# Where the merge-gate blocks stand in a hybrid attention and mLSTM layer: beside attention, or behind the mLSTM

## The chip, the cores and the metric

The kernel runs on one core of one Trainium2 chip. The metric is the device time of one execution in microseconds; of several executions the median is given. Times below come from the profile of one execution, the rows of its trace, and the list of timed runs.

## What is computed

One trunk layer on 1024 prompt tokens and 32 sample tokens, together T = 1056, with D = 1024. The normalised input `h` is multiplied by one wide weight `w_in`; its columns are the attention's q, k, v (8 heads of 64), the mLSTM's q, k, v and output gate (4 heads of 128), eight scalar gates, and the two merge gates `ga` and `gm` of 1024 columns each:

```python
h = rmsnorm(x, g_mix) * (1 + sc1) + sh1
u = h @ w_in
qa, ka, va, qm, km, vm, om, ip, fp, ga, gm = jnp.split(u, _split_points(), axis=-1)
ya = band_attention(qa, ka, va, rel_bias)        # own 64-frame chunk and the 8 before
hm, (C1, n1, m1) = mlstm_chunkwise(q_m, k_m, v_m, log_i, log_f, C0, n0, m0, block)
ym = head_rmsnorm(hm, mh_gain) * jax.nn.sigmoid(om)
merged = jax.nn.sigmoid(ga) * (ya @ w_br_att) + jax.nn.sigmoid(gm) * (ym @ w_br_mlstm)
x = x + gt1 * (merged @ w_out)
```

A SwiGLU FFN and a final norm follow. `ga` and `gm` depend on `h` alone and are first used in the merge, so their columns can be computed at any time between the first norm and the merge.

## The kernel before

**Tiling.** `h` is held transposed in eight tiles of 128 channels x 1056 tokens. All products are done in fp32 split into a high and a low part: three passes (high x high, low x high, high x low), so a *block* of 128 output columns costs 8 x 3 matmuls for each of three token ranges of 352, 72 matmuls. `unit` (line 451) issues the 24 of one range; its matmuls are line 458. A block also loads 512 KB of weights on the SP queue (L434), splits them into high (ACT, L424) and low parts (L425), and empties three PSUM tiles (pool `mm`, three buffers) on ACT. The engine of the low split is chosen in `weight` (line 427 on): POOL until the second mLSTM has opened its output tile (`hm_n[1]`), DVE from then on. Weights are loaded and split ahead by the class `Weights`: up to two blocks split ahead, three more loaded.

**The order.** The order of the instructions on PE, ACT, DVE and POOL is that of the program's text; only DMA queues are ordered by the framework. A list `segs` (line 1330) holds segments; each has blocks, which are PE's steady filler, and at most one *side job*, a generator whose steps are put between the filler's matmuls. `unit` calls `side.tick()` after every second contraction slice, that is after every six matmuls, four ticks a unit and twelve a block. A job of n steps is spread evenly: `job = side.start(gen(), steps, ticks - delay - 4, delay)`, where `ticks` is 4 x the units of the segment's blocks, and `delay` is 13 from the sixth segment on (mLSTM and later) and 0 before. A step runs when its share of the ticks has come, whatever the engines do at that time. A second queue, `side.later`, holds short tails (transposes of k and v for their outputs, splits of the mLSTM's value weights), one of which is issued at each of three places in a unit.

**The segments.** The first computes k, v, q of head pair 0. In the next three, `attention(0)` to `attention(2)` run beside the blocks k, v, q of the next pair and beside merge-gate blocks: two, two and four of the sixteen. The fifth has `attention(3)` beside the mLSTM's first value block and four convolution blocks, the sixth the first half of the mLSTM beside five more, and the last has the second half of the mLSTM, the convolution's output rows and then `branch_operands` (sigmoid gating of the mLSTM output, split of both branches' operands) beside four output-gate blocks and the other eight merge-gate blocks. The merge follows. Another job, `ada_rest` (160 steps over 495 ticks from the second segment on), computes the later modulations on DVE (L1227, L1229), one tile of `w_ada` after the other.

**A step of attention.** `attention` (line 718) works on 18 items of one pair, two heads x (eight tiles of 128 queries and one sample tile), in 22 steps: one for the low part of the queries (L643, DVE), then a software pipeline. In a step, in this order: transposes of the item two back (PE, L774, tile `psT`) and their high part (ACT, L781); scores of the item (PE, L747, tile `psS`), the pass that adds the bias and takes the maximum (DVE, L761), the exponential (ACT, L762); the low part of the transposed item (DVE, L786); the reciprocal (DVE, L766) and the normalisation (POOL, L767); the values of the item three back (PE, L805, tile `psV`), and after each second item their sum (ACT L811, DVE L812 and L813). `psS`, `psT` and `psV` are one PSUM tile each, so the next transposes wait for the low part before, and the next scores for the pass before. The tiles are 128, 256, 384, 512 and then four times 640 keys wide, and 160 for the sample.

**A gate block.** `gate_block` (line 670) is one block whose three results go raw to a tile `t` (ACT, L677; a pool of four) and then by DMA to `g_d` in HBM (L678, SP). The merge reads them back (L1582, L1583) and takes the sigmoids.

**Slots.** Sixteen slots hold all the large tiles: eight are `h`; one each the cached keys and the low queries; k, q and v of each pair take three while their attention runs. `vm_block` (line 872) takes one for its raw weights and two for their parts, which four pieces on ACT (L888) and POOL (L889) fill from `side.later`.

Of the kernel before, what the change touches and what calls it, by code (L numbers as in the profile page):

```python
# [139 lines left out]
def hybrid_stream_step(  # L140
# [37 lines left out]
    def slot(shape, dt=F32):  # L178
        return slots.tile(shape, dt, tag="s", name=nm("s"))

    def tmpt(shape=(P, T), dt=F32):
        return tmp.tile(list(shape), dt, tag="t", name=nm("t"))

    def mmt():
        return mm.tile([P, 512], F32, tag="mm", name=nm("mm"))
# [236 lines left out]
    def split_to(dst, src, eng=dve):  # L422

        act.activation(dst[:, 0], src, AF.Copy)  # L424
        eng.tensor_tensor(dst[:, 1], src, f(dst[:, 0]), op=ALU.subtract)  # L425
# [25 lines left out]
    def unit(w, w0, xt, lo, hi, last=True):  # L451

        wt = W.use(w)
        pt = mmt()
        n = len(xt)
        for k in range(n):
            for q, (a, b) in enumerate(PASSES):
                pe.matmul(pt[:, :hi - lo], wt[(w0 + k) // 4][:, a, (w0 + k) % 4], xt[k][:, b, lo:hi],  # L458
                          start=(k == 0 and q == 0), stop=(k == n - 1 and q == 2))
            if k % 2 == 0 and k:  # L460
                side.flush(1)
            if k % 2 == 1:
                side.tick()
        if last:
            W.used(w)
        return pt[:, :hi - lo]
# [86 lines left out]
    def w_cols(c0, home=None):  # L553
        return weight([w_in[:, c0:c0 + P]], KD, 3, home)
# [4 lines left out]
    def k_block(hp):  # L559
        w = w_cols(KA + hp * P)  # L560

        def run():
            kt = att_k[hp] = slot([P, 2, T], F32R)
            kf = ap_.tile([P, T - 512], F32, tag="kf", name=nm("kf"), bufs=1)
            for lo, hi, pt in units(w):

                for hh, (u, v) in enumerate(ROWS):
                    act.activation(kt[u, hh, lo:hi], pt[u], AF.Copy)
                a = max(lo, 512)
                if a < hi:  # L570
                    act.activation(kf[:, a - 512:hi - 512], pt[:, a - lo:], AF.Copy)
                for hh, (u, v) in enumerate(ROWS):
                    dve.tensor_tensor(kt[v, hh, lo:hi], pt[u], f(kt[u, hh, lo:hi]), op=ALU.subtract)
            W.advance()
            side.later += [lambda: None, lambda: k_tail(hp, kf), lambda: sample_tail(kf[:, 512:], new_k_s, hp)]
        run.w = w
        return run
# [20 lines left out]
    def v_block(hp):  # L598
        w = w_cols(VA + hp * P)

        def run():
            vf = tmpt()
            if hp == 0:
                ckv = cache_loads()
            for lo, hi, pt in units(w):
                act.activation(vf[:, lo:hi], pt, AF.Copy)
            W.advance()
            side.later += [lambda: v_tail(hp, vf, 0), lambda: None, lambda: v_tail(hp, vf, 1), lambda: None,
                           lambda: v_sample(hp, vf)]
            if hp == 0:  # L610
                side.later.append(lambda: cache_kv(ckv))
        run.w = w
        return run
# [56 lines left out]
    def gate_block(g, j):  # L670
        w = w_cols((GA, GM)[g] + j * P)

        def run():
            raw = tmpt()
            for lo, hi in TILES:
                pt = unit(w, 0, hs, lo, hi)
                act.activation(raw[:, lo:hi], pt, AF.Copy)  # L677
            sp.dma_start(g_d[2 * j + g], raw)  # L678
        run.w = w
        return run  # L680
# [155 lines left out]
    ATT_STEPS = 22  # L836
# [364 lines left out]
    ML_STEPS = 2 * (NB + 3) + 2  # L1201
# [56 lines left out]
    def om_block(b):  # L1258
        w = w_cols(OM + b * P)

        def run():
            if b % 2 == 0:
                om[b // 2] = slot([P, 2, T])
            for lo, hi in TILES:
                pt = unit(w, 0, hs, lo, hi)
                act.activation(om[b // 2][:, b % 2, lo:hi], pt, AF.Copy)
        run.w = w
        return run

    def branch_operands():  # L1270
        for b in range(4):
            o = om[b // 2][:, b % 2]
            act.activation(o, o, AF.Sigmoid)
            dve.tensor_tensor(o, o, hm_n[b // 2][:, b % 2], op=ALU.mult)
            y = slot([P, 2, T], F32R)
            yield
            split_to(y, o)
            ym.append(y)
            yield
        if "ym" in dbg:  # L1280
            for h in range(MH):
                sp.dma_start(dbg["ym"][h], om[h // 2][:, h % 2])
        for b in range(4):
            raw = tmpt()
            sp.dma_start(raw, ya_d[b])
            y = slot([P, 2, T], F32R)
            split_to(y, raw)
            ya.append(y)
            yield

    BR_STEPS = 12

    def chain(*gens):
        for g in gens:
            yield from g


    def b_qkv(hp):
        return [k_block(hp), v_block(hp), q_block(hp)]
# [3 lines left out]
    def b_gates(a, b):  # L1303
        return [gate_block(g, j) for g, j in gates[a:b]]

    def mix(a, b):

        out = []
        for i, x in enumerate(a):
            out.append(x)  # L1310
            out += b[i * len(b) // len(a):(i + 1) * len(b) // len(a)]
        return out
# [7 lines left out]
    def conv_rows():  # L1320
        yield
        pt = mmt()
        pe.transpose(pt[:48, :P], ncv, ident)
        ncr = tmpt((48, P))
        dve.tensor_copy(ncr, pt[:48, :P])
        sp.dma_start(new_conv_p[0, 0].rearrange("j (r c) -> (j r) c", c=P), ncr[0:24])
        sp.dma_start(new_conv_s[0, 0].rearrange("j (r c) -> (j r) c", c=P), ncr[24:48])

    nothing = lambda: None
    segs = [  # L1330
        (nothing, b_qkv(0), None, 0),
        (nothing, mix(b_qkv(1), b_gates(0, 2)), lambda: attention(0), ATT_STEPS),
        (nothing, mix(b_qkv(2), b_gates(2, 4)), lambda: attention(1), ATT_STEPS),
        (conv_state, b_qkv(3) + b_gates(4, 8), lambda: attention(2), ATT_STEPS),
        (mlstm_setup, [vm_block(0), conv_block(0), conv_block(4), conv_block(1), conv_block(5)],
         lambda: attention(3), ATT_STEPS),
        (open_mls, [vm_block(1), conv_block(2), conv_block(6), conv_block(3), conv_block(7)],
         lambda: mlstm(0), ML_STEPS),
        (nothing, [om_block(b) for b in range(4)] + b_gates(8, 16),
         lambda: chain(mlstm(1), conv_rows(), branch_operands()), ML_STEPS + BR_STEPS + 3),  # L1340
    ]

    for _, blocks, _, _ in segs:
# [431 lines left out]
    for pi, tiles in enumerate(parts):  # L1775
        if pi == 1:
            job = side.start(second_norm(parts[0]), 15, 50)
        for j in range(KD):
# [21 lines left out]
            a, b = tiles[0][0], tiles[-1][1]  # L1800
# [494 lines left out]
```

## Time and profile before

| | |
|---|---|
| median of 3 runs | 1607.51 us (1606.27 to 1607.71) |
| the profiled execution, first to last instruction | 1604.4 us |
| PE busy | 1576.2 us, 98% |
| DVE, ACT, POOL busy | 1135.5 (71%), 786.2 (49%), 445.3 us (28%) |
| DMA, mean | 120 GB/s |

The page names groups of instructions by line, engine, operation and tiles. PE is TensorE's matmuls and PEld its weight loads, DVE is VectorE, ACT ScalarE, POOL GpSimd, SP the queue that issues DMAs. A timeline row gives start, duration, engine, line, operation, output tile and inputs, shapes, and the count of merged instructions; in square brackets stands how long the engine was idle before, and what released it. A row of the table by stage gives the stretch, its length, the busy time of each engine with its count of instructions, the granted TensorE clock (1.00 is full), the share of the DMA engines, and GB/s.

### The profile page before, as it was taken

How to read it: one execution, taken by the hardware profiler on the slowest of the kernel's cores; microseconds unless marked ns; L12 is line 12 of the kernel's file. 1: busy time of each engine (PE TensorE's matmuls, PEld its weight loads, DVE VectorE, ACT ScalarE, POOL GpSimd, SP SyncE). 2: the span in 40 equal slices, each digit the busy share in tenths (PEclk: the TensorE clock that was granted, in tenths of full speed). 3: DMA queues.
4: the chain of work that ended last, by engine and by line, in shares of the span. 5: the costliest groups of instructions: out<-in, count | busy, mean ns of one | idle time of the engine just before them, and what ended most of it. 6: DMA issues, size and time to landing. Idle time of an engine off the chain costs nothing.

```text
span 1604.4 us, 27406 instructions
## 1 busy us (share of the span) xinstructions
PE 1576.2 (98%) x10256; PEld 1554.8 (97%) x10256; DVE 1135.5 (71%) x2185; ACT 786.2 (49%) x1747; POOL 445.3 (28%) x477
## 2 busy tenths in 40 slices
PE   7999999999999999999999999999999999999997
PEld 6989999999999999999999999999999999999997
DVE  7766564646776855556654699988888986799754
ACT  3665463544455644444443655554544444545443
POOL 2344243433332411000012100566565650000001
PEclk9999999999999999999999999999999999999999
DMA  9823323232222232675353311313222227427453
GB/s 362 273 77 91 97 82 102 88 122 86 67 80 80 69 95 69 121 276 168 121 153 113 106 54 48 100 55 105 81 79 94 67 82 252 135 79 250 135 156 126
DMA packets 210414, 192.45 MB, mean 120 GB/s; under 512 B 10706, under 2 KB 180618, under 8 KB 209258
## 3 DMA queue, kind: packets, MB, share of 16 engines
q1 hardware_dynamic: 205386, 187.82, 37.4%
q10 hardware_dynamic: 4640, 2.82, 0.6%
q8 instruction: 81, 1.33, 0.4%
q14 instruction: 51, 0.42, 0.1%
q0 software_dynamic: 256, 0.06, 0.0%
HBM read 152.19 MB, written 41.63 MB: 121 GB/s over the span
## 4 chain that ended last, share of the span: by engine, by line
PE 88%; DVE 5%; DMA 3%; ACT 2%; issue 1%; SPq 0%; ACTq 0%; POOL 0%; DVEq 0%; POOLq 0%
PE mm L458 39%; PE psb L1843 18%; PE mm L1843 10%; PE mm L2246 3%; PE mm L906 3%; PE psb L2246 2%; PE psV L805 2%; PE psb L2089 2%; PE psS L747 1%; DMA s<-in_w_ada_dram 1%; PE psT L774 1%; PE mm L2089 1%; DMA wraw<-in_w_in_dram 1%; DMA t<-in_x_sample_dram 1%; DVE s L390 1%
## 5 line engine op out<-in xcount | busy, mean ns | idle before, releaser
L458 PE MATMUL mm<-s,wsp 128*128 128x352 f32 x4104 | 689.1, 324 | 0.0
L458 PEld LDWEIGHTS mm<-s,wsp 128*128 128x128 f32 x4104 | 656.9, 188 | 2.0 <-issue 0.4
L425 DVE TENSOR_TENSOR wsp<-wraw,wsp 128x512 fp32r<-128x512 f32 (+1 forms) x280 | 234.9, 855 | 120.0 <-ACT wsp L424 118.0
L1843 PE MATMUL psb<-s,wsp 128*128 128x352 f32 x1611 | 271.7, 322 | 1.5 <-DVE wsp L425 0.8
L424 ACT ACTIVATE wsp<-wraw 128x512 fp32r<-128x512 f32 x336 | 199.5, 617 | 141.5 <-PE psb L1843 44.0
L1843 PEld LDWEIGHTS psb<-s,wsp 128*128 128x128 f32 x1611 | 260.6, 188 | 2.1 <-DVE wsp L425 1.1
L1843 PE MATMUL mm<-s,wsp 128*128 128x352 f32 x933 | 159.3, 322 | 0.0
L1843 PEld LDWEIGHTS mm<-s,wsp 128*128 128x128 f32 x933 | 151.2, 188 | 0.5 <-DVE wsp L425 0.5
L767 POOL TENSOR_SCALAR st<-st,mx 128x640 f32<-128x640 f32 (+5 forms) x72 | 55.7, 774 | 184.8 <-DVE mx L766 170.5
L1229 DVE SCALAR_TENSOR_TENSOR t<-wa,cmix,t 128x512 f32<-128x512 f32 x112 | 89.1, 801 | 15.0 <-DMA wa<-in_w_ada_dram 14.6
L425 POOL TENSOR_TENSOR wsp<-wraw,wsp 128x512 fp32r<-128x512 f32 x56 | 75.8, 1374 | 49.4 <-ACT wsp L424 47.9
L762 ACT ACTIVATE st<-st,mx 128x640 f32<-128x640 f32 (+5 forms) x72 | 47.9, 666 | 71.6 <-DVE mx L761 70.3
L761 DVE CUSTOM_DVE_ANT_0 st<-psS,bias 128x640 f32<-128x640 f32 (+5 forms) x72 | 44.3, 616 | 46.1 <-PE psS L747 33.2
L1790 POOL TENSOR_TENSOR t<-t,sl 128x352 f32<-128x352 f32 x19 | 18.3, 961 | 185.3 <-DMA wraw<-in_w_out_dram 130.8
L781 ACT ACTIVATE pT<-psT 128x640 fp32r<-128x640 f32 (+3 forms) x80 | 38.6, 493 | 63.1 <-PE psT L774 47.7
L2158 POOL TENSOR_TENSOR fst<-fst 128x1 f32<-128x1 f32 (+1 forms) x6 | 1.2, 192 | 236.6 <-ACT t L2151 236.6
L786 DVE TENSOR_TENSOR pT<-psT,pT 128x640 fp32r<-128x640 f32 (+3 forms) x80 | 43.9, 557 | 22.5 <-ACT pT L781 22.3
L1452 POOL TENSOR_TENSOR wraw<-wraw,raw 128x512 f32<-128x512 f32 x33 | 55.8, 1702 | 0.9
L906 PE MATMUL mm<-s,s 128*128 128x264 f32 (+3 forms) x432 | 54.8, 283 | 0.0
L2246 PE MATMUL mm<-s,wsp 128*128 128x352 f32 x330 | 54.4, 324 | 0.0
L2246 PEld LDWEIGHTS mm<-s,wsp 128*128 128x128 f32 x330 | 53.1, 188 | 0.0
L1452 POOL TENSOR_TENSOR spare<-wraw 128x512 f32<-128x512 f32 x11 | 16.5, 1496 | 130.0 <-DMA wraw<-in_w_gate_up_dram 122.4
(396 smaller groups left out, 2561.3 us busy)
## 6 DMA issues: line engine op xcount, KB each, us to landing
wraw<-in_w_in_dram SPq DMA_DIRECT2D x38, 512.0 KB, 4.0
wraw<-in_w_gate_up_dram SPq DMA_DIRECT2D x33, 512.0 KB, 3.8
wa<-in_w_ada_dram SPq DMA_DIRECT2D x64, 256.0 KB, 2.9
wraw<-in_w_down_dram SPq DMA_DIRECT2D x32, 512.0 KB, 4.0
a_d<-t SPq DMA_DIRECT2D x22, 528.0 KB, 2.8
g_d<-t SPq DMA_DIRECT2D x16, 528.0 KB, 3.9
x<-xres SPq DMA_DIRECT2D x16, 528.0 KB, 6.7
t<-g_d SPq DMA_DIRECT2D x16, 528.0 KB, 5.4
```

The lines of the kernel that those rows point to most:

```text
L424: act.activation(dst[:, 0], src, AF.Copy)
L425: eng.tensor_tensor(dst[:, 1], src, f(dst[:, 0]), op=ALU.subtract)
L458: pe.matmul(pt[:, :hi - lo], wt[(w0 + k) // 4][:, a, (w0 + k) % 4], xt[k][:, b, lo:hi], start=(k == 0 and q == 0), stop=(k == n - 1 and q ...
L761: dve.tensor_tensor_reduce(so, sv, bi, -1.0, 3.0e38, ALU.add, ALU.min, mx[:n, 1:2])
L762: act.activation(st[:n, :w], st[:n, :w], AF.Exp, bias=mx[:n, 1:2], scale=-1.0, accum_out=mx[:n, 2:3])
L767: pool.tensor_scalar(st[:n, :w], st[:n, :w], mx[:n, 3:4], 1.0, op0=ALU.mult, op1=ALU.mult)
L906: pe.matmul(pt[:n, :wd], hs[k][:, a, i * P:i * P + n], whl[b][:, k, :wd], start=(k == 0 and q == 0), stop=(k == KD - 1 and q == 2))
L1229: dve.scalar_tensor_tensor(ac[:, c], wa, cmix[:, c, k:k + 1], ac[:, c], op0=ALU.mult, op1=ALU.add)
L1452: self.eng.tensor_tensor(a(dst), a(x), a(y), op=op)
L1843: pe.matmul(acc, wt[:, a, k], x[k][:, b], start=(start and not onto and k == 0 and q == 0), stop=(stop and k == 3 and q == 2), skip_group_ ...
L2089: pe.matmul(acc, wt[k // 4][:, u, k % 4], piece_of[k, i][:, v], start=(k == 0 and q == 0), stop=(k == KP - 1 and q == 2))
L2246: pe.matmul(acc, wt[(k - k0) // 4][:, u, (k - k0) % 4], piece_of[k, 2][:, v], start=(k == 0 and q == 0), stop=(k == NF - 1 and q == 2))
```

## The change

Only the list of segments is changed. The three attention segments keep k, v and q of the next pair, three blocks each, and lose their gate blocks. The last segment is cut in two: the second half of the mLSTM with the convolution's rows runs beside the four output-gate blocks and the first four merge-gate blocks (29 steps), and `branch_operands` runs beside the other twelve (12 steps). The number of blocks and of ticks is the same in all; so are all shapes. The rule for the ticks is unchanged, so a side job is spread over the blocks that its own segment has now.

```diff
     segs = [
         (nothing, b_qkv(0), None, 0),
-        (nothing, mix(b_qkv(1), b_gates(0, 2)), lambda: attention(0), ATT_STEPS),
-        (nothing, mix(b_qkv(2), b_gates(2, 4)), lambda: attention(1), ATT_STEPS),
-        (conv_state, b_qkv(3) + b_gates(4, 8), lambda: attention(2), ATT_STEPS),
+        (nothing, b_qkv(1), lambda: attention(0), ATT_STEPS),
+        (nothing, b_qkv(2), lambda: attention(1), ATT_STEPS),
+        (conv_state, b_qkv(3), lambda: attention(2), ATT_STEPS),
         (mlstm_setup, [vm_block(0), conv_block(0), conv_block(4), conv_block(1), conv_block(5)],
          lambda: attention(3), ATT_STEPS),
         (open_mls, [vm_block(1), conv_block(2), conv_block(6), conv_block(3), conv_block(7)],
          lambda: mlstm(0), ML_STEPS),
-        (nothing, [om_block(b) for b in range(4)] + b_gates(8, 16),
-         lambda: chain(mlstm(1), conv_rows(), branch_operands()), ML_STEPS + BR_STEPS + 3),
+        (nothing, [om_block(b) for b in range(4)] + b_gates(0, 4),
+         lambda: chain(mlstm(1), conv_rows()), ML_STEPS + 3),
+        (nothing, b_gates(4, 16), branch_operands, BR_STEPS),
     ]
```

With `ATT_STEPS` 22, `ML_STEPS` 26, `BR_STEPS` 12. In the three attention segments the ticks over which 22 steps are spread go from 56, 56 and 80 to 32 each; the mLSTM's second half goes from a share of 41 steps in 127 ticks to 29 in 79, and the branch operands to 12 in 127.

## The prediction

> **What bounds the kernel now.** I read the page's table of busy time first, then the same table cut into stages, the list of waits of TensorE (PE) in the attention stages, and the timeline of single attention steps. From the page:
>
> ```profile
> span 1604.4 us, 27406 instructions
> PE 1576.2 (98%) x10256; PEld 1554.8 (97%) x10256; DVE 1135.5 (71%) x2185; ACT 786.2 (49%) x1747; POOL 445.3 (28%) x477
> ```
>
> PE is busy for all but 28 us. The matmuls are the same before and after, so a gain can only come from those 28 us, and a loss only from new holes. The table by stage shows the first, second and third attention, the first mLSTM, and then the second mLSTM with gates and branch operands; its first pairs are length, PE, weight loads, VectorE (DVE), ScalarE (ACT), GpSimd (POOL).
>
> ```profile
> 88.00:165.00 77.00, 74.59 (x501) 71.38 (x500) 48.74 (x123) 43.29 (x101) 30.70 (x39) 1.00 0.28 82
> 175.00:250.00 75.00, 74.39 (x503) 71.90 (x503) 47.49 (x121) 41.87 (x100) 29.01 (x36) 1.00 0.28 84
> 262.00:356.00 94.00, 93.46 (x629) 91.79 (x628) 51.63 (x128) 47.77 (x111) 34.24 (x39) 1.00 0.32 96
> 460.00:520.00 60.00, 60.00 (x473) 59.80 (x472) 41.51 (x96) 31.03 (x88) 18.68 (x28) 1.00 0.33 97
> 520.00:716.00 196.00, 196.00 (x1288) 192.96 (x1288) 114.35 (x240) 94.41 (x236) 30.37 (x51) 1.00 0.45 119
> ```
>
> PE has no hole at all from 460 to 716 us, where the gate blocks go. Where they come from it has 2.41, 0.61 and 0.54 us, together 3.56. So the change has 3.56 us to win in these stages, and it takes away what covers the attention. PE's waits from 60 to 460 us (total, times, longest):
>
> ```profile
> PE psT L774 <- DVE pT L786: 1.3, 2, 1.0
> PE psT L774 <- POOL wsp L425: 0.9, 1, 0.9
> PE psS L747 <- DVE mx L761: 0.9, 2, 0.4
> ```
>
> The cover is thin at one place: the transposes (L774) wait for the low part (L786) of the tile before, since they share one PSUM tile. One step of the first attention, full width, two ticks of filler:
>
> ```profile
> 109.46 0.73 DVE L1229 SCALAR_TENSOR_TENSOR t<-wa,cmix,t 128x512 f32<-128x512 f32 x1
> 109.71 1.15 POOL L767 TENSOR_SCALAR st<-st,mx 128x640 f32<-128x640 f32 x1 [2.32 <-DVE mx L766]
> ...
> 111.47 0.83 PE L747 MATMUL psS<-s,s 128*128 128x320 f32 x4
> ...
> 112.44 0.82 DVE L761 CUSTOM_DVE_ANT_0 st<-psS,bias 128x640 f32<-128x640 f32 x1 [2.25 <-PE psS L747]
> ...
> 112.61 2.09 PE L458 MATMUL mm<-s,wsp 128*128 128x352 f32 x12
> ...
> 113.19 0.82 DVE L786 TENSOR_TENSOR pT<-psT,pT 128x640 fp32r<-128x640 f32 x1
> ...
> 114.54 0.71 PE L774 MATMUL psT<-ident,st 128*128 128x128 f32 x5
> 114.60 0.80 POOL L767 TENSOR_SCALAR st<-st,mx 128x640 f32<-128x640 f32 x1 [3.74 <-DVE mx L766]
> ...
> 116.87 0.81 DVE L786 TENSOR_TENSOR pT<-psT,pT 128x640 fp32r<-128x640 f32 x1
> ...
> 119.69 0.71 PE L774 MATMUL psT<-ident,st 128*128 128x128 f32 x5
> ```
>
> Scores end at 112.30, DVE starts on them 0.14 later, its low part ends at 114.01, and with the same handover PE could transpose at 114.15. The 12 matmuls keep it until 114.54: 0.39 to spare. They take 114.54 - 112.61 = 1.93, so a tick (six) is 0.97 us, and a block of 72 matmuls is 11.6 us. In the next step, three ticks long, the spare is 119.69 - 117.68 - 0.14 = 1.87.
>
> **The change, step by step.** *The pace.* An attention has 22 steps, spread over (12 ticks a block) - 4 ticks: 56, 56 and 80 before, 32 each now. The steps stood 2 or 3 ticks apart in the first two and 3 or 4 in the third; now they stand 1 or 2 apart. Of the gaps that end in transposes ten are one tick now. Most of these were the three-tick ones: 1.87 spare less two ticks (1.94) is about nothing, if DVE is on time. Worked from a two-tick step instead, 0.39 less one tick leaves 0.58 short. In five of the ten short gaps a wide tile's scores stand ahead, in two of them a wide tile's low part too; the chain is shorter with the tile, so I charge 0.58 twice and half of it three times: 2.0 us for one attention (0.4 by the first way, 2.9 if all five are full).
>
> *What else DVE does.* The second attention starts like this:
>
> ```profile
> 173.51 2.53 DVE L643 TENSOR_TENSOR s<-t,s 64x1056 fp32r<-64x1056 f32 x2
> ...
> 174.21 0.93 ACT L568 ACTIVATE s<-mm 64x352 fp32r<-64x352 f32 x2 [2.79 <-PE mm L458]
> ...
> 175.95 0.34 PE L747 MATMUL psS<-s,s 128*128 128x128 f32 x2
> 176.06 1.06 DVE L573 TENSOR_TENSOR s<-mm,s 64x352 fp32r<-64x352 f32 x2
> ...
> 177.15 0.49 DVE L1227 TENSOR_SCALAR t<-wa,cmix 128x512 f32<-128x512 f32 x1
> 177.67 0.29 DVE L761 CUSTOM_DVE_ANT_0 st<-psS,bias 128x128 f32<-128x128 f32 x1
> ```
>
> The K block's low halves (1.06, behind 0.93 of ACT) and the modulation sums stand ahead of the scores' pass, which starts 1.38 after the scores end. That was covered by two or three ticks. A K block ends three units; a short gap is met half the time, so 3 x 0.7 = 2.1 (0 to 4.2). The V block's splits, the value sums and the modulation come in the same way:
>
> ```profile
> 114.67 0.42 DVE L812 TENSOR_TENSOR t<-psV,t 64x256 f32<-64x256 f32 x1 [0.24 <-ACT t L811]
> 115.12 0.42 DVE L813 TENSOR_TENSOR t<-psV,t 64x256 f32<-64x256 f32 x1
> 115.47 0.73 DVE L1229 SCALAR_TENSOR_TENSOR t<-wa,cmix,t 128x512 f32<-128x512 f32 x1
> ...
> 120.04 0.69 DVE L622 TENSOR_TENSOR s<-mm,s 128x512 fp32r<-128x512 f32 x1 [1.30 <-ACT s L619]
> ```
>
> The second stage falls from 75 to 75 - 2 x 11.6 = 52 us; DVE's 47.49 lose 24 ticks of modulation (24 x 160/495 = 7.8 steps of 0.73, 5.7 us) and stay at 41.8, 80% of the stage against 63%. Four collisions of a value pair with one of the others, 0.5 each, make 2.0 (an estimate; 0 to 5). Together 6.1 us an attention, 18.3 in three.
>
> *The query's low half.* The first scores follow the step with L643 by one tick where they followed by three. They need the first of the two (1.26 with 0.14 of handover), so PE waits 0.43, in the second and third attention: 0.9 (3.4 if both halves are waited for).
>
> *POOL at the end of the third attention.* PE in the second head of the second attention, before and after; psS are scores, psV values, mm filler (three matmuls a row), psT transposes:
>
> ```order
> L747 MATMUL psS_2554<-s_885,s_735 128x320
> L805 MATMUL psV_2566<-pT_2507,s_1273 128x256 x3
> L458 MATMUL mm_2540<-s_531,wsp_2236 128x352 x3
> L458 MATMUL mm_2540<-s_558,wsp_2236 128x352 x3
> L458 MATMUL mm_2540<-s_585,wsp_2237 128x352 x3
> L458 MATMUL mm_2540<-s_611,wsp_2237 128x352 x3
> L458 MATMUL mm_2540<-s_638,wsp_2237 128x352 x3
> L458 MATMUL mm_2540<-s_675,wsp_2237 128x352 x3
> L774 MATMUL psT_2591<-ident,st_2513 128x128 x5
> ```
>
> ```order
> L747 MATMUL psS_2184<-s_885,s_735 128x320
> L805 MATMUL psV_2196<-pT_2143,s_1465 128x256 x3
> L458 MATMUL mm_2212<-s_449,wsp_1906 128x352 x3
> L458 MATMUL mm_2212<-s_497,wsp_1906 128x352 x3
> L774 MATMUL psT_2219<-ident,st_2149 128x128 x5
> ```
>
> Eighteen filler matmuls became six: that is the pace above. On POOL, at the third attention's last normalisations (L767), before and after:
>
> ```order
> L767 TENSOR_SCALAR st_3739<-st_3739,mx_3740 128x640
> L767 TENSOR_SCALAR st_3799<-st_3799,mx_3800 128x640
> L767 TENSOR_SCALAR st_3855<-st_3855,mx_3856 32x160
> L889 TENSOR_TENSOR s_3891<-s_3358,s_3890 128x528 x4
> L862 MEMSET tri 128x128
> ```
>
> ```order
> L767 TENSOR_SCALAR st_2981<-st_2981,mx_2982 128x640
> L767 TENSOR_SCALAR st_3019<-st_3019,mx_3020 128x640
> L889 TENSOR_TENSOR s_2998<-s_2207,s_2997 128x528 x2
> L767 TENSOR_SCALAR st_3063<-st_3063,mx_3064 128x640
> L889 TENSOR_TENSOR s_2998<-s_2207,s_2997 128x528
> L767 TENSOR_SCALAR st_3097<-st_3097,mx_3098 32x160
> ```
>
> The splits of the mLSTM's value weights (L889) came behind the last normalisation; now two stand ahead of the last but one. Their tile takes the slot of the third attention's queries, which is free only after the last scores. POOL has waited there before, with nothing behind it:
>
> ```profile
> L889 POOL TENSOR_TENSOR s<-s,s x8: 1282/1308/1853, 354.7 to 457.3; 128x528 fp32r<-128x528 f32 x4, 128x512 fp32r<-128x512 f32 x4
> ...
>   PE psV L805: 7.6, 1
> ```
>
> Now PE's transposes of that tile wait: 2 x 1.31 + 0.80 + about 0.4 of handovers = 3.8 after the last scores, against values and 12 matmuls, about 2.4 (2.24 in the step quoted, which had a value matmul less). That is 1.4, or 2.8 at 1.85 and 1.15. The long normalisation above (1.15) lies over DVE's L1229, which reads two SBUF tensors; the short one (0.80) over L812, which reads one and PSUM. [...] I take 1.4, since beside attention only the modulation and the queries' low half have that form.
>
> *Where the gates go.* Eight blocks bring to the late stages their 512 KB loads and 528 KB stores on SP, three evacuations each on ACT, and 16 splits that move from POOL (1.37 each) to DVE (0.86):
>
> ```profile
> L425 DVE TENSOR_TENSOR wsp<-wraw,wsp 128x512 fp32r<-128x512 f32 (+1 forms) x280 | 234.9, 855 | 120.0 <-ACT wsp L424 118.0
> L425 POOL TENSOR_TENSOR wsp<-wraw,wsp 128x512 fp32r<-128x512 f32 x56 | 75.8, 1374 | 49.4 <-ACT wsp L424 47.9
> ```
>
> That is 14 us on a DVE that was busy 114.35 of 196: nothing. The second mLSTM runs 29 steps in 79 ticks (0.37 a tick, was 41 in 127, 0.32); the first ran 26 in 67 (0.39) without a hole: nothing. The branch operands get 127 ticks for 12 steps; the last still comes shortly before the merge: nothing.
>
> *Sum.* 18.3 + 0.9 + 1.4 = 20.6, so a span of 1625.0. The span was 1604.4 where the median time is 1607.51, so 3.1 lie around it: 1628.1 us.
>
> **The rivals.** *Hidden after all* (0.08). If DVE is on time everywhere, the three-tick rows hold: 0.4 in each attention, and 1.4 on POOL: about 1610. For it: 1.87 spare in the step quoted. Against: 1.38 of lateness at the K block.
> *Faster* (0.05). POOL loses 16 splits (a wait of 0.9 was theirs), and the holes of the three stages close: 1607.5 - 3.6 = 1603.9. It decides if the low part is ready within one tick at full width; 0.58 short speaks against it.
> *The chain sets the pace* (0.12). All five wide gaps pay 0.58, every K unit 1.4, the rest 5: 12.1 an attention, 36.3, with 3.4 and 2.8: 1650. It holds if DVE, which must take a step's work in order behind ACT's exponentials, falls a full instruction behind at each short gap.
> *The clock falls* (0.01). [...] Granted clock is 1.00 in all stages, with holes of at most 1.0. [...]
>
> **How the numbers follow.** My forecast, 1628, has 0.74. Its lower end takes 0.4 an attention plus half of the K term (1.1), 0.9 and nothing on POOL: 1607.5 + 5.4 = 1613; I set 1612. The upper end is that of the paced chain less a part: 1648. Outside lie the faster and hidden cases and some of the paced one. A measurement here can tell about 0.2% (3.2 us) from no change: faster 0.05, same 0.08, slower 0.74 + 0.12 + 0.01 = 0.87.
>
> **What would show it.** Right: PE's idle in the three attention stages rises from 3.6 to some 20 us, mostly psT waiting for DVE's pT; DVE about 80% busy there; one POOL wait at the end of the third; stages after it without holes. Wrong: no such waits, or holes from the second mLSTM to the merge, or waits on ACT, weights or DMA instead.

## The result, and the profile after

The changed kernel takes 1655.22 us (median of 4 runs, 1654.59 to 1655.73) against 1607.24 us of the kernel before on the same chip (4 runs, 1606.27 to 1607.71): a ratio of 1.0299, 95% interval 1.0285 to 1.0314, or 48.0 us. It is slower, as predicted, and by more than the range allowed (1612 to 1648; predicted 1628.1).

The page of the kernel after, its span and busy times, and of the part in 40 slices the rows of PE and of the granted clock:

```profile
span 1653.7 us, 27417 instructions
PE 1593.9 (96%) x10256; PEld 1564.6 (95%) x10256; DVE 1138.6 (69%) x2201; ACT 786.2 (48%) x1747; POOL 422.8 (26%) x461
PE   7988888899999999999999999999999999999997
PEclk9999899999999999999999999999999999999999
```

The span is 49.3 us longer. PE's idle time, span less busy time, went from 28.2 to 59.8 us, 31.6 more; and PE was *busy* 17.7 us longer with the same 10256 matmuls. So something other than holes is in it: the matmuls took longer. The table by stage says where. The first three rows are the three attentions, then come the stages that have gained the gates (length, PE, weight loads, DVE, ACT, POOL, granted clock, DMA share, GB/s):

```profile
85.00:155.00 70.00, 60.16 (x392) 55.00 (x391) 48.57 (x122) 40.38 (x96) 23.82 (x33) 0.98 0.21 60
155.00:232.00 77.00, 66.13 (x416) 60.77 (x415) 45.60 (x119) 39.25 (x96) 26.65 (x36) 0.93 0.24 68
232.00:320.00 88.00, 75.27 (x476) 69.63 (x475) 51.84 (x126) 44.91 (x107) 34.13 (x41) 0.94 0.20 60
460.00:520.00 60.00, 60.00 (x402) 58.52 (x401) 46.87 (x98) 34.99 (x97) 21.08 (x36) 1.00 0.34 76
520.00:716.00 196.00, 196.00 (x1276) 194.42 (x1275) 87.40 (x193) 74.29 (x184) 15.23 (x27) 1.00 0.38 109
```

PE has 9.8, 10.9 and 12.7 us of holes in the three attentions, against 2.4, 0.6 and 0.5 before, and none where the gates went. The granted clock, 1.00 in all five rows of the kernel before, is 0.98, 0.93 and 0.94 there. PE's waits from 60 to 460 us (total, times, longest):

```profile
PE psS L747 <- DVE mx L761: 12.8, 7, 2.3
PE psT L774 <- DVE pT L786: 12.2, 15, 2.4
PE psV L805 <- DVE t L813: 7.8, 12, 2.6
PE psT L774 <- DVE mx L766: 1.1, 2, 0.6
PE psT L774 <- POOL st L767: 0.9, 1, 0.9
```

Together 34.8 where the same waits were 3.0 before (1.3 for the low part, 0.9 for the pass, and the row here):

```profile
PE psV L805 <- DVE t L813: 0.8, 4, 0.2
```

That is the idle time that was added. The wait that the prediction expected most of, psT for the low part (L786), is a third of it. The next scores' wait for the pass before (psS for L761) and the next values' wait for the pair's sum (psV for L813) come to more, and the prediction names neither among the waits that would show it right.

One of the long holes, at the end of the first head of the first attention, as the timeline shows it (start, duration, engine, line, operation, shapes; in brackets the idle time before and what ended it):

```profile
110.00 0.82 PE L747 MATMUL psS<-s,s 128*128 128x320 f32 x4
...
111.10 1.06 DVE L573 TENSOR_TENSOR s<-mm,s 64x352 fp32r<-64x352 f32 x2 [0.56 <-ACT kf L571]
...
112.17 1.34 DVE L1229 SCALAR_TENSOR_TENSOR t<-wa,cmix,t 128x512 f32<-128x512 f32 x1
...
113.54 0.82 DVE L761 CUSTOM_DVE_ANT_0 st<-psS,bias 128x640 f32<-128x640 f32 x1
...
114.29 0.82 DVE L786 TENSOR_TENSOR pT<-psT,pT 128x640 fp32r<-128x640 f32 x1
...
115.25 1.30 PE L774 MATMUL psT<-ident,st 128*128 128x128 f32 x5 [2.35 <-DVE pT L786]
```

The scores are there at 110.82. DVE first takes the keys' low halves (waiting 0.56 for ACT's copy), then a step of the modulation, which took 1.34 where the median of its 112 is 0.74 (the only two of 1.34 are the two that had two of POOL's weight splits beside them), then the scores' pass, then the low part. PE stands 2.35 us. When it goes on, five transposes take 1.30 us; they took 0.71 before. And the start of the second attention:

```profile
158.59 3.00 POOL L664 TENSOR_SCALAR s<-s 64x352 fp32r<-64x352 f32 x2 [2.28 <-ACT s L662]
160.39 0.33 PE L747 MATMUL psS<-s,s 128*128 128x128 f32 x2
...
161.68 2.50 POOL L425 TENSOR_TENSOR wsp<-wraw,wsp 128x512 fp32r<-128x512 f32 x2
164.12 0.14 POOL L714 MEMSET bias<- 64x64 f32 x1
164.29 0.29 DVE L761 CUSTOM_DVE_ANT_0 st<-psS,bias 128x128 f32<-128x128 f32 x1 [3.05 <-POOL bias L714]
...
164.65 0.50 PE L747 MATMUL psS<-s,s 128*128 128x256 f32 x2 [1.95 <-DVE mx L761]
```

The first scores need a mask that POOL writes into the bias tile (L714), and POOL has two copies of the queries (L664, 3.00) and a block's weight split (L425, two instructions, 2.50) ahead of it. DVE waits 3.05, PE 1.95; at the starts of the second, third and fourth attention DVE waits 9.5 for these masks. The prediction did not look at this wait. At the fourth attention's start, where no gate block was taken away, it costs PE 1.86, and the last stretch at half clock (326.7) follows it.

**The clock.** The clock's records in the two traces hold two values, 1.00 and 0.50. They show six stretches at half clock in the kernel after, 27.3 us together, and none in the kernel before, leaving out, here and below, one that starts 5 to 7 us before the end of every kernel. Their starts (115.1, 166.3, 193.6, 244.8, 309.6 and 326.7 us) lie whole multiples of 3.413 us apart (62 of them from the first to the last) and their lengths are one or two times 3.41. Cut along that grid, the table of one window and the next, twice:

```profile
87.76:91.17 3.41, 1.74 (x12) 1.45 (x11) 2.79 (x6) 1.01 (x4) 2.16 (x4) 1.00 0.07 7
91.17:94.59 3.42, 2.06 (x12) 1.69 (x11) 2.30 (x7) 1.58 (x5) 0.67 (x2) 1.00 0.50 146
111.65:115.06 3.41, 1.25 (x10) 0.95 (x8) 3.36 (x5) 1.70 (x3) 2.96 (x2) 1.00 0.00 0
115.06:118.48 3.42, 3.23 (x16) 3.22 (x17) 1.42 (x6) 2.31 (x7) 0.90 (x2) 0.50 0.77 209
```

A window in which PE was busy for 1.74, just over half, is followed by full clock; one with 1.25 is followed by 0.50. At half clock twelve filler matmuls, from 169.28 to the transposes at 172.80, take 3.52 us; in the kernel before, from 112.61 to 114.54, they take 1.93. By these rows 45% of the busy time at half clock is lost. PE was busy for 24.0 of the 27.3 us, so some 10.8 us of busy time come from it (an estimate from these rows): three fifths of the 17.7.

### The profile page after: what moved, and what is told of

It is laid out like the page before. It is cut to its first block, busy times and chain, and to the rows that moved or that the text cites. A ratio compares the mean times of both kernels' runs of the same rounds, so it can differ in the third digit from the quotient of the medians.

```text
span 1653.7 us, 27417 instructions
## 1 busy us (share of the span) xinstructions
PE 1593.9 (96%) x10256; PEld 1564.6 (95%) x10256; DVE 1138.6 (69%) x2201; ACT 786.2 (48%) x1747; POOL 422.8 (26%) x461
## 4 chain that ended last, share of the span: by engine, by line
PE 83%; DVE 6%; DMA 4%; ACT 3%; issue 1%; POOL 1%; SPq 0%; ACTq 0%; DVEq 0%; POOLq 0%
PE mm L458 37%; PE psb L1844 17%; PE mm L1844 10%; PE mm L2247 3%; PE mm L906 3%; PE psb L2247 2%; PE psb L2090 2%; DVE st L761 2%; DMA xres<-s 1%; PE psS L747 1%; DMA s<-in_w_ada_dram 1%; PE psT L774 1%; PE psV L805 1%; PE mm L2090 1%; ACT st L762 1%
## 5 line engine op out<-in xcount | busy, mean ns | idle before, releaser
L458 PEld LDWEIGHTS mm<-s,wsp 128*128 128x128 f32 x4104 | 662.4, 190 | 2.1 <-issue 0.4
L425 DVE TENSOR_TENSOR wsp<-wraw,wsp 128x512 fp32r<-128x512 f32 (+1 forms) x296 | 244.4, 844 | 144.2 <-ACT wsp L424 142.2
L1844 PEld LDWEIGHTS mm<-s,wsp 128*128 128x128 f32 x933 | 151.2, 188 | 0.5 <-DVE wsp L425 0.3
L767 POOL TENSOR_SCALAR st<-st,mx 128x640 f32<-128x640 f32 (+5 forms) x72 | 50.1, 695 | 167.1 <-DVE mx L766 138.6
L1229 DVE SCALAR_TENSOR_TENSOR t<-wa,cmix,t 128x512 f32<-128x512 f32 x112 | 84.1, 766 | 11.0 <-DMA wa<-in_w_ada_dram 10.6
L761 DVE CUSTOM_DVE_ANT_0 st<-psS,bias 128x640 f32<-128x640 f32 (+5 forms) x72 | 44.4, 616 | 44.8 <-PE psS L747 24.3
L677 ACT ACTIVATE t<-mm 128x352 f32<-128x352 f32 x48 | 22.2, 463 | 107.5 <-PE mm L458 103.2
L425 POOL TENSOR_TENSOR wsp<-wraw,wsp 128x512 fp32r<-128x512 f32 x40 | 53.1, 1348 | 32.1 <-ACT wsp L424 17.9
L747 PE MATMUL psS<-s,s 128*128 128x320 f32 (+2 forms) x192 | 45.5, 346 | 12.8 <-DVE mx L761 12.8
L906 PEld LDWEIGHTS mm<-s,s 128*128 128x128 f32 (+1 forms) x432 | 53.5, 185 | 0.5
```

The source lines that it names most:

```text
L747: pe.matmul(sc[:, o:o + b - a], x[:, hh, q0:q0 + P], kt[:, hh, k0 + a:k0 + b], start=(i == 0), stop=(i == 1))
L761: dve.tensor_tensor_reduce(so, sv, bi, -1.0, 3.0e38, ALU.add, ALU.min, mx[:n, 1:2])
L767: pool.tensor_scalar(st[:n, :w], st[:n, :w], mx[:n, 3:4], 1.0, op0=ALU.mult, op1=ALU.mult)
L906: pe.matmul(pt[:n, :wd], hs[k][:, a, i * P:i * P + n], whl[b][:, k, :wd], start=(k == 0 and q == 0), stop=(k == KD - 1 and q == 2))
L1229: dve.scalar_tensor_tensor(ac[:, c], wa, cmix[:, c, k:k + 1], ac[:, c], op0=ALU.mult, op1=ALU.add)
L1844: pe.matmul(acc, wt[:, a, k], x[k][:, b], start=(start and not onto and k == 0 and q == 0), stop=(stop and k == 3 and q == 2), skip_group_ ...
```

## The experiments

**Theory A**, formed on these rows: with one or two ticks between steps each instruction that stands in order ahead of the one PE waits for makes a hole of its own: on DVE the keys' low halves, the modulation and the pair's sums, on POOL the weight split ahead of the masks; and where a window of 3.41 us is less than about half busy, the next runs at half clock. **Theory B**: the steps stand too close, and their own chain (scores, pass, exponential, normalisation, transposes, low part) is too long, whatever else DVE does. As to the clock, the **rival** is that the length of a hole alone decides, wherever it lies. The kernel before stood between 1606.27 and 1606.34 us on the chips of these runs, and differences are taken from that. The kernel after was not timed again beside them; its 1655.2 is carried over, and `att_only`, the same in the attention half, gave 1655.16 there. Counted so, the loss is 48.8 to 48.9 us in place of 48.0.

**Which half of the change it is.** The attention half alone: all sixteen gates in one last segment.

```diff
-        (nothing, [om_block(b) for b in range(4)] + b_gates(0, 4),
-         lambda: chain(mlstm(1), conv_rows()), ML_STEPS + 3),
-        (nothing, b_gates(4, 16), branch_operands, BR_STEPS),
+        (nothing, [om_block(b) for b in range(4)] + b_gates(0, 16),
+         lambda: chain(mlstm(1), conv_rows(), branch_operands()), ML_STEPS + BR_STEPS + 3),
```

> Only the attention half of the change: no gate block beside attention, all sixteen in one last segment whose job is the second mLSTM, the convolution's rows and the branch operands in one chain, as before the change. If the loss of 48 us sits in the three attention stages alone (as the trace after the change has it: PE waits for DVE there, and six stretches at half clock), the time stays at 1655, within 3. If the cut of the last segment, or the branch operands spread over 127 ticks, carry a part, it falls by that part, to 1650 or less.

Measured: 1655.16 us, ratio 1.0304 (1.0288 to 1.0319), idle 58.3, 23.9 us at half clock. The whole loss is there.

The late half alone: merge-gate blocks beside attention as before, the last segment cut in two.

```diff
-        (nothing, [om_block(b) for b in range(4)] + b_gates(8, 16),
-         lambda: chain(mlstm(1), conv_rows(), branch_operands()), ML_STEPS + BR_STEPS + 3),
+        (nothing, [om_block(b) for b in range(4)] + b_gates(8, 12),
+         lambda: chain(mlstm(1), conv_rows()), ML_STEPS + 3),
+        (nothing, b_gates(12, 16), branch_operands, BR_STEPS),
```

> Only the late half: attention keeps its 2, 2 and 4 gate blocks, and the last segment is cut in two, the second mLSTM beside four output-gate and four merge-gate blocks, the branch operands beside the last four. If the loss is all in attention: 1607, within 2. If the cut of the last segment costs or gains by itself: off by 3 or more.

Measured: 1610.52 us (1608.04 to 1613.35), ratio 1.0024 (1.0012 to 1.0035): 4.2 us slower, where none was expected if all the loss is in attention. Here only four gate blocks are left beside the branch operands, and the merge finds its operands late (the profiled execution took 1612.79):

```profile
718.00:724.00 6.00, 3.92 (x25) 3.62 (x23) 0.70 (x2) 1.92 (x4) 0.00 (x0) 1.00 0.90 325
724.00:731.00 7.00, 5.91 (x20) 5.92 (x21) 4.27 (x9) 2.07 (x6) 0.00 (x0) 0.51 0.51 165
```

The kernel after, with twelve blocks there, has no hole from 500 to 760 us, so this loss belongs to the short segment and not to the change.

**How much cover is missing.** One gate block given back to each attention (44 ticks instead of 32; 56, 56 and 80 before).

```diff
-        (nothing, b_qkv(1), lambda: attention(0), ATT_STEPS),
-        (nothing, b_qkv(2), lambda: attention(1), ATT_STEPS),
-        (conv_state, b_qkv(3), lambda: attention(2), ATT_STEPS),
+        (nothing, mix(b_qkv(1), b_gates(0, 1)), lambda: attention(0), ATT_STEPS),
+        (nothing, mix(b_qkv(2), b_gates(1, 2)), lambda: attention(1), ATT_STEPS),
+        (conv_state, b_gates(2, 3) + b_qkv(3), lambda: attention(2), ATT_STEPS),
...
```

The other thirteen stay in the last two segments.

> The changed kernel with one gate block given back to each of the three attentions, so 22 steps in 44 ticks instead of 32; the other thirteen stay late. A loss in proportion to the ticks taken away (36 of the 96 come back) would give 1655 - 18 = 1637. If a part of the loss is the clock, which falls to half after a window of 3.4 us in which PE was busy less than about half, one tick more a step closes the worst holes first, so the clock part (some 14) goes whole and half of the holes: about 1625.

Measured: 1615.01 us, ratio 1.0055 (1.0040 to 1.0070), idle 34.9, no half clock. A step every two ticks costs 8.7 us, a step every one and a half 48. Three of the eight blocks bring back 39 of the 48 us; the loss is nothing like proportional, and lower than either number expected.

**What stands ahead on DVE.** The modulation started only with the fifth segment, behind these attentions.

```diff
-        if i == 1:
-            ada = side.start(ada_rest(), ADA_STEPS, 495)
+        if i == 4:
+            ada = side.start(ada_rest(), ADA_STEPS, 387)
```

> The changed kernel, with the modulation job (0.73 us of DVE a step) started at the fifth segment over 387 ticks instead of at the second over 495, so that the first three attentions have none of it. Theory A: PE waits because DVE, in order, has the K block's low halves, the modulation and the value sums ahead of the scores' pass; about 12 steps fewer in each attention take a third of the holes (some 10 us) and with them half of the stretches at half clock (some 7): about 1638. Theory B: the bare chain (scores, pass, low part, transposes) is too long for one tick whatever else DVE does: 1652 or more.

Measured: 1641.46 us, ratio 1.0220 (1.0205 to 1.0235), idle 49.3, 17.1 us at half clock: 13.8 us gone, of them 10.5 idle: 3.5 us above theory A's number, and 10 below theory B's.

The keys' low halves filled by POOL with zeros in place of DVE's subtraction (L573).

```diff
-                    dve.tensor_tensor(kt[v, hh, lo:hi], pt[u], f(kt[u, hh, lo:hi]), op=ALU.subtract)
+                    pool.tensor_scalar(kt[v, hh, lo:hi], f(kt[u, hh, lo:hi]), 0.0, 0.0, op0=ALU.mult, op1=ALU.mult)
```

> The kernel after, with the low halves of the keys (L573) not computed: POOL fills them with zeros instead, so DVE loses an instruction of about 1.06 us ahead of the scores' pass at the end of every unit of a K block, six in an attention's stage, and the keys' low part is missing from the scores. Theory A (DVE's ordered other work makes the holes, and the clock falls in a window of 3.41 us in which PE is less than about half busy): PE's idle time goes from 60 to about 50, two or three of the six half-clock stretches go, about 1640 us. Theory B (the bare chain of one-tick steps is too long, whatever else DVE does): idle at least 56, 1650 or more.

Measured: 1634.82 us, ratio 1.0177 (1.0162 to 1.0192), idle 45.7, 6.8 us at half clock in the attentions: 20.4 us gone, the largest single part, 5 us more than theory A gave; POOL has more work in exchange. The same place in this kernel:

```profile
106.13 0.82 PE L747 MATMUL psS<-s,s 128*128 128x320 f32 x4
...
106.59 0.73 DVE L1229 SCALAR_TENSOR_TENSOR t<-wa,cmix,t 128x512 f32<-128x512 f32 x1
...
107.25 0.81 DVE L761 CUSTOM_DVE_ANT_0 st<-psS,bias 128x640 f32<-128x640 f32 x1
...
109.86 0.74 PE L774 MATMUL psT<-ident,st 128*128 128x128 f32 x5 [0.80 <-DVE mx L766]
```

The pass starts 0.30 behind the end of the scores where it started 2.72 behind, the hole is 0.80 for 2.35, and the transposes run at full clock (0.74).

**What stands ahead on POOL.** The bias tile and masks of an attention's first head issued at the end of its query block.

```diff
+            early[2 * hp] = rel_bias_tile(2 * hp)
         run.w = w
...
-                bts[hh] = rel_bias_tile(2 * hp + hh)
+                bts[hh] = early.pop(2 * hp + hh, None) or rel_bias_tile(2 * hp + hh)
```

> The kernel after, with the bias tile and masks of the next attention's first item issued on POOL one block earlier, ahead of the weight splits behind which they stood. Theory A: the two waits of the scores' pass for POOL's mask (5.5 us in two) go, and with them about 4 us of PE's idle time and about 3 us of half clock: about 1648 us. Theory B: POOL plays no part, 1653 or more.

Measured: 1643.89 us, ratio 1.0234 (1.0219 to 1.0249), idle 52.4, 17.1 us at half clock: 11.3 us gone, where theory A gave 7: two mask instructions of 0.14 and 0.15 in each attention now come earlier, and the load of their tile with them. The start of the second attention now:

```profile
160.14 0.33 PE L749 MATMUL psS<-s,s 128*128 128x128 f32 x2
161.29 0.15 POOL L716 MEMSET bias<- 64x64 f32 x1
161.47 0.29 DVE L763 CUSTOM_DVE_ANT_0 st<-psS,bias 128x128 f32<-128x128 f32 x1 [0.47 <-POOL bias L716]
161.72 2.52 POOL L425 TENSOR_TENSOR wsp<-wraw,wsp 128x512 fp32r<-128x512 f32 x2
162.29 0.40 PE L749 MATMUL psS<-s,s 128*128 128x256 f32 x2
```

The mask stands ahead of the split, and the second scores (162.29) wait for nothing.

**The pair's sums.** L812 and L813 left out in the first three attentions, so that their output holds one of the three products of probabilities and values.

```diff
-                dve.tensor_tensor(y, q4[:DH, :, 0], y, op=ALU.add)
-                dve.tensor_tensor(y, q4[:DH, :, 1], y, op=ALU.add)
+                if hp == 3:
+                    dve.tensor_tensor(y, q4[:DH, :, 0], y, op=ALU.add)
+                    dve.tensor_tensor(y, q4[:DH, :, 1], y, op=ALU.add)
```

> The kernel after, with the two sums on DVE behind each pair of items (L812, L813) left out in the first three attentions, so that the output holds only one of the three products of probabilities and values: ACT's copy alone empties the tile psV. Theory A (each hole is some instruction of DVE's that stands in order): psV's waits, 7.8 us in 12, go nearly whole, and with them one or two of the six half-clock stretches: idle some 50 to 53, 1638 to 1645 us. Rival (psV's wait only hides another that ends as late): idle 57 or more, 1651 or more.

Measured: 1646.49 us, ratio 1.0254 (1.0237 to 1.0271), idle 53.3, 20.5 us at half clock in the attentions: 8.7 us gone; the time is 1.5 us above the expected range. psV's waits for the sum are gone, but the next ones on DVE grew a little (psT for the low part from 11.9 to 13.2 us, psS from 10.9 to 12.6, from 85 to 320 us).

**What is left without all these.** Keys' low halves zero, masks early, modulation late, in one kernel; and the same without the pair's sums.

> The kernel after, with the keys' low halves left out as above, the masks issued early as above, and the modulation begun only at the fifth segment: the steps of attention one or two ticks apart as in the kernel after, but DVE with little besides them. Theory A: PE idle some 36 to 42, at most one half-clock stretch, 1612 to 1622 us. Theory B: the steps alone keep PE waiting, idle 48 or more, 1635 or more.

> The same taken out of the kernel with bare steps (keys' low halves zero, masks early, modulation from the fifth segment on), which stood at 1626.8 with 5.2 us of waits of psV, 3.5 for the reciprocal, 2.9 for POOL's normalisation, 2.1 for the scores' pass and 1.7 for the low part. Theory A: 1619 to 1622, no half clock. If it is below 1612, the pair's sums also made the other waits; if above 1625, the chain of a step sets the pace whatever DVE does.

Measured: 1626.78 us, ratio 1.0127 (1.0110 to 1.0144), idle 41.5, and 1620.15 us, ratio 1.0086 (1.0071 to 1.0101), idle 40.1; no half clock in either. The first is 5 us above theory A's range and 8 below theory B's: both had a part. The second is in its range. PE's longest waits in it (its line numbers are two higher than those of the kernel after):

```profile
PE psT L776 <- DVE pT L788: 5.3, 14, 1.0
PE psT L776 <- DVE mx L768: 3.8, 5, 0.9
PE psT L776 <- POOL st L769: 3.0, 3, 1.0
PE psS L749 <- DVE mx L763: 2.1, 2, 1.7
```

These are mainly the chain of a step itself: low part, reciprocal, normalisation, none over 1.0 us (the last row has one wait of 1.7). This kernel stands 13.8 us above the kernel before. The values' low halves (L622) and the queries' (L643) are still on its DVE, so 13.8 is the most that the chain alone costs. The other 35 us hang on what DVE and POOL do besides, with the clock's fall that comes of it.

**The clock by itself.** The kernel before with a hole made on PE at the start of each of the twelve blocks of the last segment: transposes, n copies on ACT one behind the other, a transpose of the last copy; n is 2 and 4. Nothing of the attentions is touched. (The tile `junk` is made once, outside of the lines shown.)

```diff
+    def hole():
+        pt = mmt()
+        for i in range(4):
+            pe.transpose(pt[:, i * P:(i + 1) * P], ident, ident)
+        for _ in range(n):
+            act.activation(junk, pt, AF.Copy)
+        pt = mmt()
+        pe.transpose(pt[:, :P], junk[:, 384:512], ident)
+        act.activation(junk[:, :16], pt[:, :16], AF.Copy)
```

> The kernel before, with a hole made on PE at the start of each of the last segment's twelve blocks: four transposes, two copies of their tile on ACT one behind the other, and a transpose that needs the last copy. Holes of about 1.4 us, where nothing else waits. [...]

> The same with four copies on ACT, so holes of about 2.6 us. Theory A (half clock after a window of 3.41 us on a fixed grid in which PE is less than about half busy): some 8 or 9 of the 12 holes fall so that a window is below half, about 29 us at half clock, which cost 15: 12 x (2.6 + 0.7) + 15 = 55, about 1662 us. [...]

Measured, short: 1640.08 us, ratio 1.0209 (1.0192 to 1.0226). Twelve holes of 1.4 us, with 0.7 for the transposes of each, would make 25 us, about 1632 (an estimate from the times above). The waits are a little longer than meant (1.7 on average for 1.4), and three windows did fall to half clock, where holes of 1.4 would have left each window 0.59 busy or more (2.01 of 3.41):

```profile
PE mm L682 <- ACT junk L680: 20.0, 12, 2.1
```

The longest of these holes is 2.1 us. Along the grid, a window that held a whole hole of 2.0, and one with 1.5 us of a hole of 1.7:

```profile
618.19:621.60 3.41, 1.37 (x11) 1.13 (x9) 0.00 (x0) 2.96 (x9) 0.00 (x0) 1.00 0.05 16
621.60:625.02 3.42, 3.42 (x14) 3.42 (x13) 2.80 (x6) 0.67 (x2) 0.00 (x0) 0.50 0.23 36
679.63:683.04 3.41, 1.95 (x13) 1.93 (x14) 0.85 (x2) 2.96 (x8) 0.87 (x2) 1.00 0.81 168
683.04:686.45 3.41, 3.41 (x23) 3.41 (x22) 2.94 (x6) 0.69 (x2) 0.00 (x0) 1.00 0.68 32
```

The window 0.40 busy (1.37 of 3.41) is followed by half clock, the one 0.57 busy by full clock. Its span is 34.1 us longer, 19.8 idle and 14.3 busy; of the busy time 4.6 is 45% of the 10.2 us at half clock, which leaves 9.7 for the 60 extra transposes.

Measured, long: 1666.56 us, ratio 1.0375 (1.0360 to 1.0391). Nine stretches of half clock, 37.5 us together, where theory A had 29. The holes came out longer than meant:

```profile
PE mm L682 <- ACT junk L680: 35.1, 12, 3.4
```

Five are of 3.0 us or more, but five of the nine stretches follow holes of 2.6 to 3.0. And one of the long ones speaks against the rival. The hole of 3.15 us from 555.8 on is cut by the grid, and both windows are followed by full clock:

```profile
554.16:557.57 3.41, 1.61 (x13) 1.35 (x11) 2.47 (x5) 2.61 (x6) 1.51 (x2) 1.00 0.03 10
557.57:560.98 3.41, 2.06 (x13) 2.07 (x14) 1.61 (x2) 2.85 (x6) 1.43 (x3) 1.00 0.36 77
```

So a hole of 3.15 us left the clock full, and three of 2.0 did not. The sum 35.1 + 9.7 + 0.45 x 37.5 = 62 is close to the 60.3 measured.

**Can it beat the kernel before?** Both exact edits on the kernel before, in three builds.

> The kernel before, with both exact edits (masks early, modulation from the fifth segment on). The three attention stages had 3.6 us of holes; 0.9 of them waited for POOL's weight split, the rest for DVE. Theory A: up to 2 us faster, 1605 to 1607. Rival: the modulation, now denser in the last segments, makes new holes before the merge: 1609 or more.

> The kernel before with the masks issued early and nothing else. Its attention stages had no wait for the masks, only 0.9 us for a weight split on POOL. Theory A: at most 1 us faster, 1605.5 to 1606.5, a difference below what can be told. Rival (the early masks cost something by themselves on POOL or in their buffers): 1608 or more.

> The kernel before with the masks early and the modulation spread over the 291 ticks that are left from the fifth segment on, where the earlier build had 387 and left two tiles over for the merge. Theory A: 1604 to 1606, since the attention stages have 3.6 us of holes to win. Rival (160 steps in 291 ticks crowd DVE in the later segments): 1609 or more, with holes after 420 us.

Measured: 1637.57 us for the first, ratio 1.0195 (1.0180 to 1.0211). The 387 ticks are those of the kernel after; the kernel before has 291 left from there, so that the modulation was unfinished at the merge, where PE waited 32.2 us for it. That is a fault of the edit and says nothing on the attentions. Masks early alone: 1605.94 us, ratio 0.9997 (0.9988 to 1.0006), no difference, as expected. With the modulation over 291 ticks: 1620.74 us, ratio 1.0089 (1.0076 to 1.0103), slower, as the rival had it. From 60 to 320 us PE's idle time fell from 3.8 to 1.2 us, as theory A had it, but behind it came new holes:

```profile
60.00:320.00 260.00, 258.77 (x1716) 251.46 (x1716) 122.38 (x315) 141.19 (x330) 93.02 (x125) 1.00 0.27 81
320.00:420.00 100.00, 97.74 (x700) 95.28 (x699) 61.16 (x164) 41.75 (x103) 34.12 (x47) 1.00 0.30 93
420.00:500.00 80.00, 74.58 (x544) 71.92 (x544) 64.94 (x137) 39.46 (x89) 25.35 (x36) 0.98 0.30 90
```

No version here beats the kernel before.

## Why the prediction failed, step by step

**Where and in which direction: right.** The loss is in the three attentions (but for one mask wait of 1.86 and a window at half clock at the start of the fourth), the engine that PE waits for is DVE, and the stages that take the gates have no hole (196.00 of 196.00). "DVE about 80% busy there" was too much: it is 69%, 59% and 59% of the three rows above. The 52 us behind the 80% were taken from a cut of 75 us that leaves out the end of the stage: the second attention's first scores start at 176.0 in the kernel before and the third's at 262.5, 86.5 us apart, so that 63 were to be expected; it came out at 77.6. The 3.1 us set around the span were too many as well: an execution of the kernel before of 1606.42 us has a span of 1604.4.

**The pace, priced at 6.0 in three attentions: too small.** The kernel with bare steps and no sums stands 13.8 us above the kernel before. In that stand also the terms for the queries' low half (0.9) and for POOL's end (1.4), so the predicted 8.3 is to be set against 13.8. The 0.9 came to nothing: no wait of PE's from 60 to 460 us is put down to L643. The step charged PE for the low part alone (5.3 here); the reciprocal (3.8 in five waits) and POOL's normalisation (3.0 in three) together cost more.

**What else DVE does, 6.3 for the keys and 6.0 for the rest: the failed step.** It priced the keys' low halves at 0.7 a unit, half of a delay of 1.38 that was read where two or three ticks covered it. Taken out, they bring 20.4 us. The modulation brings 13.8 and the sums 8.7, each taken out alone; the three cannot be added, since in bare steps sums bring 6.6, and keys, masks and modulation together 28.4 and not 45.5. Against the 12.3 of this step stand 35.0 us that go, with the clock's fall that comes of them, when keys, modulation, sums and masks are all taken out. The timeline at 110 us shows how the delays come one behind the other. The keys' halves stand behind ACT's copies, the modulation behind them and stretched by POOL, and only then come the two instructions that PE waits for. A chance of one half for each collision, taken by itself, leaves this out. That it is so at the other holes too is argued from this place and from the runs that take one part out; no run shows it hole by hole.

**POOL: right at the end, not seen at the start.** The order foreseen at the third attention's end is there, and cost 0.9 where 1.4 was priced:

```profile
297.57 2.61 POOL L889 TENSOR_TENSOR s<-s,s 128x528 fp32r<-128x528 f32 x2 [3.57 <-ACT s L888]
300.16 0.80 POOL L767 TENSOR_SCALAR st<-st,mx 128x640 f32<-128x640 f32 x1
...
301.02 0.77 PE L774 MATMUL psT<-ident,st 128*128 128x128 f32 x5 [0.95 <-POOL st L767]
```

The same question at an attention's start had no term. There the mask, 0.14 us of work, stands behind 5.5 us on POOL (second attention), and over three attentions, the second to the fourth, cost 11.3 with what followed.

**The clock: the rival with a chance of 0.01 came true in part.** The step sets a granted clock of 1.00 and holes of at most 1.0 against it, and the sum has no term for it; no run shows a length of hole from which on the clock falls. Waits of 1.9 to 2.6 us were enough, and in the experiment holes of 2.0, while one of 3.15 was not. In the trace of the kernel after the stretches at half clock (granted 0.50) are of 3.41 and 6.83 us on one grid, each behind a window of 3.41 us in which PE was 0.36 to 0.47 busy: windows here and there, 27.3 us together, not whole stages. So the loss is made of 31.6 us of idle time, where 20.6 were predicted, and of 17.7 us of busy time, where none was. Without the 10.8 of half clock the kernel would stand near 1644, inside the range; that is worked out and was not run.

Neither theory holds alone. Bare steps cost at most 13.8 us, the pair's sums 6.6 on top of them, and keys, modulation and masks with the clock's fall the other 28.4 (48.8 together, counted from the kernel before beside these runs). How much of the 28.4 each would have at full clock stays open, since each of them also decides which windows fall. Open also are 6.9 us of PE's longer busy time that half clock doesn't explain (17.7 less 10.8).

## What to carry to other kernels

When filler is taken from beside a chain, go through every in-order queue that the chain crosses and add up all that can stand ahead of the awaited instruction at once, not each delay by itself with a chance; a memset of 0.14 us, behind 5.5 us of POOL's other work, kept DVE waiting for 3.05. Then look at PE's busy share in windows of 3.41 us: in the traces of these sixteen kernels, from 60 us on, each one at full clock that was 0.45 busy or less was followed by one at half clock, and none of 0.52 or more was. With both, the price of thin cover rose here far more than in proportion: a step every two ticks cost 8.7 us, every one and a half 48, and of what lies between in the two profiles 25 us are idle time and 15 busy time.

## What the hardware showed beside that

Cut along the grid of 3.41 us, the sixteen kernels' traces hold 41 windows at full clock that were followed by half clock, 0.51 busy at most (the kernel after has six of them, 0.36 to 0.47 busy); counted are those from 60 us on, without the last stretch before each kernel's end. In that part every window at full clock that was 0.45 busy or less was followed by half clock, none of 0.52 or more was; between them (0.46 to 0.51) both were seen. Before 60 us the share does not decide alone: in the first 4 us windows of 0 to 0.40 left the clock full, and one window 0.81 busy, at 37.75 us of the kernel without the pair's sums, was followed by half clock; why stays open.

A window already at half clock kept the next one at half when it was up to 0.79 busy (one even at 0.91), and brought full clock back from 0.84 on. So by its busy time PE has to be busier to get the clock back than to keep it; by the work done it is not so, since 0.84 of a window at half clock is, at 3.52 us for what takes 1.93, the work of 0.46 at full clock. At 244.8 us of the kernel after, 0.88 us of idle time in a window at half clock (0.74 busy) was enough to keep the next at half too. That a second hole right behind the first costs more than the first follows from this only as an estimate; no run tries it by itself.
